# Both token tiles of a head in one pass through the attention, and one 256-column matmul for both parts of v

## The chip, the cores and the metric

The kernel runs on one core of one Trainium2 chip. The metric is the device time of one execution in microseconds; the median of three runs before the change is 2178.97 us (2178.82 to 2180.45).

## The reference

Two layers of a decoder over 256 tokens of 2048 features, in float32. Each layer runs an attention group and a convolution group side by side from one projection, joins them with one output projection, and ends in an MLP with a squared ReLU:

```python
for l in range(2):
    h = rmsnorm(x, attn_norm_g[l])
    q, k, v, gate_b, gate_c, conv_in = split(h @ w_in[l], ...)   # six parts of 1024 columns
    q, k = rmsnorm(q per map of 64), rmsnorm(k per map of 64)    # 8 heads, 2 maps each
    # differential attention of one head, blocks of 128 queries:
    s = (q_m . k_m) * scale + bias        # for both maps m, causal mask
    p = softmax(s[0]) - lam * softmax(s[1])
    attn = p @ v                          # v: 256 keys x 128
    attn = rmsnorm(attn, subln_g[l]) * (1 - lam_init)
    conv = gate_b * causal_conv3(gate_c * conv_in, conv_w[l])
    x = x + concat([attn, conv]) @ w_out[l]
    x = x + relu(rmsnorm(x) @ w_up[l])**2 @ w_down[l]
```

## The kernel before

Activations lie in SBUF in two token tiles of 128 tokens (`NT = 2`). Every float32 operand of a large matmul is split into a high part and a low part, and a product is made of three matmuls: high by high, high by low, low by high (`TERMS`). Weights stream in as `raw` tiles on SP's queue; ScalarE writes the high part (`whi`, line 282), VectorE the low part (`wlo`, line 283). `Weights.take` makes them three uses ahead.

TensorE runs in the order of the program (a manual schedule); the other engines' orders are settled by a scheduler when the program is built. The long stream on TensorE is the projections: in each layer q, k, v for heads 0 to 3 (512 columns each), q, k, v for heads 4 to 7, then gc and ci in turn (the convolution's inputs, four times 256 columns, `linear_t`, in which the weights stand still and high and low activations stream past in one 512-column matmul), then gb, then the output projection o. Between every few of these matmuls the code calls `work.tick()`. Side work is written as Python generators that yield how many ticks to wait; `Background` advances them at the ticks. So the attention of heads 0 to 3 is issued among the projections of heads 4 to 7 and that of heads 4 to 7 among gc and ci. A tick comes every six matmuls of 512 columns in q, k and v, and every four matmuls in gc and ci, so ticks are shorter there.

`attention` (line 486) runs eight units for a group of four heads, one for each token tile `t` and head `i`, all four heads of tile 0 first, started four ticks apart by `staggered`. A unit does:

- scores: for both maps three matmuls into a PSUM bank `sc` (line 500). A map has 64 features, so map 0 uses rows 0 to 63 of the array and map 1 rows 64 to 127. Tile 0 has 128 keys, tile 1 has 256.
- VectorE adds the bias and takes the maximum (line 503); ScalarE takes the exponential (510); VectorE forms the difference of the maps, `p` (521).
- nine ticks later: TensorE transposes `p` into a bank `ptp` (526); ScalarE and VectorE write its high and low parts, `pT` (528, 529).
- four ticks later: the product with v, three matmuls of 128 columns for each block of 128 keys (536), into a PSUM tile `av` that gathers the four heads of one token tile.
- with the fourth head: `av` is copied to `ao` (544), squared sums are taken on ScalarE (`asq`, 549), GpSimd makes the norm factors (`ams`, `a_e`, `a_r`, `af`, lines 551 to 554 and the helper's 380 and 382), VectorE scales (`an`, 556); nine ticks later TensorE transposes `an` into a bank `atp` (562) and ScalarE and VectorE write the two parts into `cat` (565, 566), which o reads.

PSUM has eight banks: two double banks for the projections (`mm`), three single banks in rotation (tag `bank`: `sc`, `ptp`, `atp` and others), and one for `av`. SBUF scratch of 512 columns comes from the pool `nat` (tag `wide`, seven buffers), scratch of the attention from `tmp`. The convolution (line 573 on) uses ScalarE, VectorE (579) and GpSimd (583) in the same stretch as the second group's attention. At the end of the mixer's scope its SBUF is reused by the MLP, whose first loads of w_up (`uraw`) wait on SP's queue for it.

Of the kernel before, what the change touches and what calls it, by code (L numbers as in the profile page):

```python
# [9 lines left out]
F32 = mybir.dt.float32  # L10
F32R = mybir.dt.float32r
AF = mybir.ActivationFunctionType
ALU = mybir.AluOpType
AX = mybir.AxisListType

P = 128
DEPTH = 2
D = 2048
S = 256
NT = S // P  # L20
AW = 1024
NH = 8
DK = 64
# [5 lines left out]
CH = 512  # L29
# [8 lines left out]
TERMS = ((0, 0), (0, 1), (1, 0))  # L38
# [46 lines left out]
def staggered(pieces, apart):  # L85

    entries = [[i * apart, p] for i, p in enumerate(pieces)]
    while entries:
        for e in list(entries):
            if e[0] <= 0:  # L90
                try:
                    e[0] = max(1, next(e[1]))
                except StopIteration:
                    entries.remove(e)
                    continue
            e[0] -= 1
        if entries:
            yield 1
# [3 lines left out]
def trunk(ctx: ExitStack, tc: tile.TileContext, x, w_in, w_out, conv_w, q_norm_g, k_norm_g,  # L102
          lambda_q1, lambda_k1, lambda_q2, lambda_k2, subln_g, attn_norm_g, mlp_norm_g,
          w_up, w_down, rel_bias, selector, out):
    nc = tc.nc
# [2 lines left out]
    xpool = ctx.enter_context(tc.tile_pool(name="xpool", bufs=1))  # L108
    apool = ctx.enter_context(tc.tile_pool(name="apool", bufs=4))
    wpool = ctx.enter_context(tc.tile_pool(name="wpool", bufs=3))  # L110
    nat = ctx.enter_context(tc.tile_pool(name="nat", bufs=7))
    small = ctx.enter_context(tc.tile_pool(name="small", bufs=4))
    dram = ctx.enter_context(tc.tile_pool(name="dram", bufs=1, space=bass.MemoryType.DRAM))
    mm = ctx.enter_context(tc.tile_pool(name="mm", bufs=2, space=PSUM))
    ps = ctx.enter_context(tc.tile_pool(name="ps", bufs=3, space=PSUM))
# [6 lines left out]
    def bank(name):  # L122
        return ps.tile([P, CH], F32, tag="bank", name=name)

    def wide(name):
        return nat.tile([P, CH], F32, tag="wide", name=name)
# [18 lines left out]
    ident = const.tile([P, P], F32, tag="ident", name="ident")  # L145
# [41 lines left out]
    s_gain = const.tile([P, DEPTH], F32, tag="sg", name="s_gain")  # L187
    nlam = const.tile([P, DEPTH], F32, tag="nlam", name="nlam")
# [188 lines left out]
    def rstd_of(ss, n, name, shape):  # L377

        e = small.tile([P, shape], F32, tag="rs_e", name=f"{name}_e")
        nc.gpsimd.tensor_scalar(e, ss, 1.0 / n, EPS, op0=ALU.mult, op1=ALU.add)  # L380
        r = small.tile([P, shape], F32, tag="rs_r", name=f"{name}_r")
        nc.gpsimd.tensor_tensor(r, e, mhalf[:, :shape], op=ALU.pow)
        return r
# [101 lines left out]

    def attention(l, qT, kT, v, h0, dst, bias, tmp):

        parts = dst.open()
        avs, r0s = {}, {}

        def unit(t, i):
            W = (t + 1) * P
            h = h0 + i
            s = tmp.tile([P, 2, S], F32, tag="s", name=f"s{h}_{t}")
            mx = small.tile([P, 2], F32, tag="mx", name=f"mx{h}_{t}")
            su = small.tile([P, 2], F32, tag="su", name=f"su{h}_{t}")
            for m in range(2):
                sc = bank(f"sc{h}_{t}_{m}")
                for n, (a, b) in enumerate(TERMS):
                    nc.tensor.matmul(  # L500
                        sc[:, :W], qT[m * DK:(m + 1) * DK, a, i, t * P:(t + 1) * P],
                        kT[m * DK:(m + 1) * DK, b, i, :W], start=(n == 0), stop=(n == 2))
                nc.vector.tensor_tensor_reduce(
                    out=s[:, m, :W], in0=sc[:, :W], in1=bias[:, 2 * h + m, S - W:],
                    op0=ALU.add, op1=ALU.max, scale=1.0, scalar=-3.0e38,
                    accum_out=mx[:, m:m + 1])
            nm = small.tile([P, 2], F32, tag="nm", name=f"nm{h}_{t}")
            nc.vector.tensor_scalar_mul(nm, mx, -1.0)
            for m in range(2):
                nc.scalar.activation(s[:, m, :W], s[:, m, :W], AF.Exp, bias=nm[:, m:m + 1],  # L510
                                     accum_out=su[:, m:m + 1])
            rc = small.tile([P, 2], F32, tag="rc", name=f"rc{h}_{t}")
            nc.vector.reciprocal(rc, su)
            if i == 0:
                r0s[t] = small.tile([P, 4], F32, tag="r0", name=f"r0_{h0}_{t}")
            nc.vector.tensor_copy(r0s[t][:, i:i + 1], rc[:, 0:1])
            c = small.tile([P, 1], F32, tag="c", name=f"c{h}_{t}")
            nc.vector.scalar_tensor_tensor(c, su[:, 0:1], rc[:, 1:2], nlam[:, l:l + 1],
                                           op0=ALU.mult, op1=ALU.mult)
            p = tmp.tile([P, S], F32, tag="p", name=f"p{h}_{t}", bufs=2)  # L520
            nc.vector.scalar_tensor_tensor(p[:, :W], s[:, 1, :W], c, s[:, 0, :W],
                                           op0=ALU.mult, op1=ALU.add)
            yield 9
            tp = bank(f"ptp{h}_{t}")
            for b in range(t + 1):
                nc.tensor.transpose(tp[:, b * P:(b + 1) * P], p[:, b * P:(b + 1) * P], ident)
            pT = tmp.tile([P, 2, S], F32R, tag="pT", name=f"pT{h}_{t}", bufs=2)
            nc.scalar.activation(pT[:, 0, :W], tp[:, :W], AF.Copy)
            nc.vector.tensor_sub(pT[:, 1, :W], tp[:, :W], pT[:, 0, :W].bitcast(F32))
            yield 4  # L530
            if i == 0:
                avs[t] = ps.tile([P, CH], F32, tag="av", name=f"av{h0}_{t}", bufs=1)
            av = avs[t]
            for k in range(t + 1):
                for n, (a, b) in enumerate(TERMS):
                    nc.tensor.matmul(  # L536
                        av[:, i * P:(i + 1) * P], pT[:, a, k * P:(k + 1) * P],
                        v[:, b, k, i * P:(i + 1) * P],
                        start=(k == 0 and n == 0), stop=(k == t and n == 2))
            if i < 3:  # L540
                return
            r0 = r0s[t]
            ao = wide(f"ao{h0}_{t}")
            nc.scalar.activation(ao, av, AF.Copy)
            ss = small.tile([P, 4], F32, tag="ams", name=f"ams{h0}_{t}")
            junk = wide(f"asq{h0}_{t}")
            for b in range(4):
                c = slice(b * P, (b + 1) * P)
                nc.scalar.activation(junk[:, c], ao[:, c], AF.Square, accum_out=ss[:, b:b + 1])
            for _ in range(2):  # L550
                nc.gpsimd.tensor_tensor(ss, ss, r0, op=ALU.mult)
            f = rstd_of(ss, P, f"a{h0}_{t}", 4)
            f2 = small.tile([P, 4], F32, tag="af2", name=f"af2{h0}_{t}")
            nc.gpsimd.tensor_tensor(f2, f, r0, op=ALU.mult)
            an = wide(f"an{h0}_{t}")
            nc.vector.tensor_tensor(
                an.rearrange("p (g d) -> p g d", d=P), ao.rearrange("p (g d) -> p g d", d=P),
                f2.unsqueeze(2).to_broadcast([P, 4, P]), op=ALU.mult)
            yield 9
            tp = bank(f"atp{h0}_{t}")  # L560
            for b in range(4):
                nc.tensor.transpose(tp[:, b * P:(b + 1) * P], an[:, b * P:(b + 1) * P], ident)
            tp3 = tp.rearrange("p (h c) -> p h c", c=P)
            hi = parts[:, 0, :, t * P:(t + 1) * P]
            nc.scalar.activation(hi, tp3, AF.Copy, scale=s_gain[:, l:l + 1])
            nc.vector.scalar_tensor_tensor(
                parts[:, 1, :, t * P:(t + 1) * P], tp3, s_gain[:, l:l + 1], hi.bitcast(F32),
                op0=ALU.mult, op1=ALU.subtract)

        yield from staggered([unit(t, i) for t in range(NT) for i in range(4)], 4)  # L570
        dst.ready = True

    def conv(l, q, u, cv, norm):
# [453 lines left out]
```

## Time and profile before

| | |
|---|---|
| median of three runs | 2178.97 us (2178.82 to 2180.45) |
| the profiled execution | 2181.14 us, span of its instructions 2179.4 us |
| TensorE matmuls, weight loads | 2156.6 us (99%), 1828.6 us (84%), 11066 each |
| VectorE, ScalarE, GpSimd | 1603.9 us (74%), 1271.7 us (58%), 138.8 us (6%) |
| attention group of heads 0 to 3, first layer | among q, k, v from 84.7 to 163.8 us |
| attention group of heads 4 to 7, first layer | among gc and ci from 164 to 213.5 us |
| TensorE clock granted | 0.999 |

In the rows of the profile, PE is TensorE, PEld its weight loads, DVE VectorE, ACT ScalarE, POOL GpSimd, SP the queue that issues most loads. A row of the groups gives line, engine, operation, output<-inputs with shapes, count, then busy time in us and the mean of one in ns, then the idle time of the engine before it and what ended it. A row of the chain in order of time, or of the timeline, starts with start and duration in us. In the chain, the duration runs to the next piece; in the timeline it is the instruction's own, and matmuls overlap.

### The profile page before, as it was taken

How to read it: one execution, taken by the hardware profiler on the slowest of the kernel's cores; microseconds unless marked ns; L12 is line 12 of the kernel's file. 1: busy time of each engine (PE TensorE's matmuls, PEld its weight loads, DVE VectorE, ACT ScalarE, POOL GpSimd, SP SyncE). 2: the span in 40 equal slices, each digit the busy share in tenths (PEclk: the TensorE clock that was granted, in tenths of full speed). 3: DMA queues.
4: the chain of work that ended last, by engine and by line, in shares of the span. 5: the costliest groups of instructions: out<-in, count | busy, mean ns of one | idle time of the engine just before them, and what ended most of it. 6: DMA issues, size and time to landing. Idle time of an engine off the chain costs nothing.

```text
span 2179.4 us, 29050 instructions
## 1 busy us (share of the span) xinstructions
PE 2156.6 (99%) x11066; PEld 1828.6 (84%) x11066; DVE 1603.9 (74%) x2229; ACT 1271.7 (58%) x1718; POOL 138.8 (6%) x194
## 2 busy tenths in 40 slices
PE   8999999999999999999999999999999999999999
PEld 6888888888888888888888888888888888888887
DVE  6677655698888888855566776557988888887554
ACT  6456445566666666654454654455666666665443
POOL 2021100000000000100011111000000000001000
PEclk9999999999999999999999999999999999999999
DMA  7555656476666666587565466656766666666774
GB/s 256 180 156 177 218 185 184 157 238 223 213 212 215 220 208 214 189 277 241 175 205 181 156 199 197 184 173 190 225 218 217 213 212 216 219 208 212 246 242 145
DMA packets 292491, 446.62 MB, mean 205 GB/s; under 512 B 10403, under 2 KB 191221, under 8 KB 292352
## 3 DMA queue, kind: packets, MB, share of 16 engines
q1 hardware_dynamic: 285648, 423.66, 61.5%
q0 software_dynamic: 6656, 21.10, 2.6%
q8 instruction: 86, 1.41, 0.3%
q14 instruction: 53, 0.43, 0.1%
q10 hardware_dynamic: 48, 0.02, 0.0%
HBM read 425.84 MB, written 18.90 MB: 204 GB/s over the span
## 4 chain that ended last, share of the span: by engine, by line
PE 94%; DMA 2%; DVE 2%; ACT 1%; issue 1%; SPq 0%; DVEq 0%; ACTq 0%
PE upc L809 29%; PE dn L969 15%; PE pr L849 13%; PE o L338 8%; PE q L338 4%; PE gc L360 4%; PE ci L360 4%; PE k L338 4%; PE gb L360 4%; PE v L338 4%; PE upw L809 1%; DMA uraw<-in_w_up_dram 1%; PE sc L500 1%; PE av L536 1%; PE tpn L402 1%; DMA draw<-in_w_down_dram 1%
## 5 line engine op out<-in xcount | busy, mean ns | idle before, releaser
L283 DVE TENSOR_TENSOR wlo<-raw,whi 128x1024 fp32r<-128x1024 f32 (+1 forms) x386 | 473.3, 1228 | 385.5 <-ACT whi L282 381.0
L282 ACT ACTIVATE whi<-raw 128x1024 fp32r<-128x1024 f32 (+1 forms) x386 | 406.8, 1055 | 477.8 <-PE dn L969 166.7
L809 PE MATMUL upc<-nT,uhi 128*128 128x512 f32 x1920 | 477.5, 391 | 0.0
L694 ACT ACTIVATE uhi<-uraw 128x1024 fp32r<-128x1024 f32 x256 | 271.2, 1060 | 287.3 <-PE upc L809 253.9
L809 PEld LDWEIGHTS upc<-nT,uhi 128*128 128x128 f32 x1920 | 352.7, 188 | 68.2
L695 DVE TENSOR_TENSOR ulo<-uraw,uhi 128x1024 fp32r<-128x1024 f32 x256 | 312.8, 1222 | 115.3 <-ACT uhi L694 112.9
L969 PE MATMUL dn<-whi,g 128*128 128x512 f32 x1024 | 316.4, 389 | 0.0
L809 PEld LDWEIGHTS upc<-nT,ulo 128*128 128x128 f32 x1920 | 261.9, 190 | 18.7
L809 PE MATMUL upc<-nT,ulo 128*128 128x256 f32 x1920 | 267.7, 282 | 0.0
L969 PEld LDWEIGHTS dn<-whi,g 128*128 128x128 f32 x1024 | 192.2, 188 | 39.7
L969 PE MATMUL dn<-wlo,g 128*128 128x512 f32 x512 | 199.6, 390 | 1.1 <-DVE wlo L283 1.0
L338 PE MATMUL o<-whi,cat 128*128 128x512 f32 x512 | 159.6, 390 | 0.0
L969 PEld LDWEIGHTS dn<-wlo,g 128*128 128x128 f32 x512 | 96.1, 188 | 22.6 <-DVE wlo L283 2.8
L338 PEld LDWEIGHTS o<-whi,cat 128*128 128x128 f32 x512 | 96.2, 188 | 19.7
L338 PE MATMUL o<-wlo,cat 128*128 128x512 f32 x256 | 99.6, 389 | 0.0
L831 POOL DMA_DIRECT2D hid<-h x64 | 34.9, 545 | 949.1 <-ACT h L830 913.4
L849 PE MATMUL pr<-t13h,f 128*128 128x512 f32 x240 | 93.8, 391 | 0.0
L338 PE MATMUL q<-whi,nT 128*128 128x512 f32 x256 | 86.4, 406 | 4.1 <-ACT nT L248 4.1
L338 PE MATMUL k<-whi,nT 128*128 128x512 f32 x256 | 85.3, 399 | 0.0
L849 PE MATMUL pr<-t24h,f 128*128 128x512 f32 x240 | 84.0, 391 | 0.0
L849 PE MATMUL pr<-b2h,f 128*128 128x512 f32 x240 | 84.0, 391 | 0.0
L338 PE MATMUL v<-whi,nT 128*128 128x512 f32 x256 | 83.4, 396 | 0.0
(330 smaller groups left out, 3431.0 us busy)
## 6 DMA issues: line engine op xcount, KB each, us to landing
uraw<-in_w_up_dram SPq DMA_DIRECT2D x128, 1024.0 KB, 5.9
raw<-in_w_in_dram SPq DMA_DIRECT2D x192, 512.0 KB, 3.9
draw<-in_w_down_dram SPq DMA_DIRECT2D x64, 1024.0 KB, 5.1
raw<-in_w_down_dram SPq DMA_DIRECT2D x64, 1024.0 KB, 5.7
raw<-in_w_out_dram SPq DMA_DIRECT2D x64, 512.0 KB, 3.6
hid<-h POOLq DMA_DIRECT2D x64, 256.0 KB, 4.3
back<-hid SPq DMA_DIRECT2D x32, 512.0 KB, 3.3
rev<-by_dist_d POOLq DMA_DIRECT2D x4, 1024.0 KB, 11.1
```

Source lines behind the costliest of these rows:

```text
L282: nc.scalar.activation(hi[:, k], raw[:, k], AF.Copy)
L283: nc.vector.tensor_sub(lo[:, k], raw[:, k], hi[:, k].bitcast(F32))
L338: nc.tensor.matmul(acc[:, t], a.ap[:, pa, k % KG, t * P:(t + 1) * P], (hi, lo)[pw][:, j], start=(k == 0 and n == 0), stop=(k == nk - 1 and ...
L360: nc.tensor.matmul(acc[:, f, 0] if part else acc[:, f], wt[:, k % 4, fs], a.ap[:, 0, k % KG] if part else a.ap[:, :, k % KG], start=(part ...
L402: nc.tensor.transpose(tp[:, i * S + t * P:i * S + (t + 1) * P], xs[n][:, t, k * P:(k + 1) * P], ident)
L500: nc.tensor.matmul(sc[:, :W], qT[m * DK:(m + 1) * DK, a, i, t * P:(t + 1) * P], kT[m * DK:(m + 1) * DK, b, i, :W], start=(n == 0), stop=(n ...
L694: nc.scalar.activation(hi, src, AF.Copy)
L695: nc.vector.tensor_sub(lo, src, hi.bitcast(F32))
L809: nc.tensor.matmul(acc[:, 0] if part else acc, wt[:, k], a.ap[:, 0, k % KG] if part else a.ap[:, :, k % KG], start=(part == 0 and kh == 0 ...
L831: nc.gpsimd.dma_start(hid[i // 2][:, i % 2 * 2 * S:(i % 2 + 1) * 2 * S], u)
L849: nc.tensor.matmul(prods[n], fs[j][:, pa, a], b[pw], start=(j == 0 and m == 0), stop=(stop and m == 2))
L969: nc.tensor.matmul(acc[:, t], f[:, pa, k, t * P:(t + 1) * P], (hi, lo)[pw][:, k % 2], start=(b == 0 and k == 0 and m == 0), stop=(b == NB2 ...
```

## The change

A unit is now a head with both its token tiles: four units for a group, started eight ticks apart.

- The twelve score matmuls are issued together, the maps alternating; both tiles share the bank of their map (columns 0 to 127 tile 0, 128 to 383 tile 1). The exponentials, sums and differences are written side by side into one tile `s`, and `p` takes the place of its first map.
- One bank `ptp` takes all three transposes, and one pass each makes the high and the low part `pT`.
- The product with v: the high part of the probabilities meets both parts of v in one matmul of 256 columns, the low part meets the high part of v in one of 128. `av` holds one head: for each tile the sum and, beside it, the share of v's low part. ScalarE copies that share to `low`, VectorE adds it to the rest into `ao`.
- With the fourth head, both tiles are normalised one after the other, and nine ticks later both are transposed one after the other.
- Buffers: `nat` six and not seven, `s` two larger ones and not three, `pT` one and not two, `ao` in `tmp`; `av` one for each head.

```diff
-    nat = ctx.enter_context(tc.tile_pool(name="nat", bufs=7))
+    nat = ctx.enter_context(tc.tile_pool(name="nat", bufs=6))
...
-        def unit(t, i):
-            W = (t + 1) * P
+        OFF = (0, P)
+        r0 = small.tile([P, 4, NT], F32, tag="r0", name=f"r0_{h0}")
+        ao = tmp.tile([P, NT, CH], F32, tag="ao", name=f"ao{h0}", bufs=1)
+
+        def unit(i):
...
-            for m in range(2):
-                sc = bank(f"sc{h}_{t}_{m}")
-                for n, (a, b) in enumerate(TERMS):
...
+            sc = [bank(f"sc{h}_{m}") for m in range(2)]
+            for t in range(NT):
+                W = (t + 1) * P
+                for n, (a, b) in enumerate(TERMS):
+                    for m in range(2):
+                        nc.tensor.matmul(
+                            sc[m][:, OFF[t]:OFF[t] + W],
+                            qT[m * DK:(m + 1) * DK, a, i, t * P:(t + 1) * P],
+                            kT[m * DK:(m + 1) * DK, b, i, :W], start=(n == 0), stop=(n == 2))
...
             yield 9
-            tp = bank(f"ptp{h}_{t}")
-            for b in range(t + 1):
+            tp = bank(f"ptp{h}")
+            for b in range(3):
                 nc.tensor.transpose(tp[:, b * P:(b + 1) * P], p[:, b * P:(b + 1) * P], ident)
...
             yield 4
-            for k in range(t + 1):
-                for n, (a, b) in enumerate(TERMS):
-                    nc.tensor.matmul(
-                        av[:, i * P:(i + 1) * P], pT[:, a, k * P:(k + 1) * P],
-                        v[:, b, k, i * P:(i + 1) * P],
-                        start=(k == 0 and n == 0), stop=(k == t and n == 2))
+            av = ps.tile([P, CH], F32, tag="av", name=f"av{h}", bufs=1)
+            av = av.rearrange("p (t n c) -> p t n c", t=NT, n=2)
+            for t in range(NT):
+                for k in range(t + 1):
+                    w = slice(OFF[t] + k * P, OFF[t] + (k + 1) * P)
+                    nc.tensor.matmul(av[:, t], pT[:, 0, w], v[:, :, k, i * P:(i + 1) * P],
+                                     start=(k == 0), stop=False, skip_group_check=True)
+                    nc.tensor.matmul(av[:, t, 0], pT[:, 1, w], v[:, 0, k, i * P:(i + 1) * P],
+                                     start=False, stop=(k == t), skip_group_check=True)
+            low = nat.tile([P, NT, P], F32, tag="wide", name=f"avl{h}")
+            nc.scalar.activation(low, av[:, :, 1], AF.Copy)
+            nc.vector.tensor_add(ao[:, :, i * P:(i + 1) * P], av[:, :, 0], low)
             if i < 3:
                 return
...
+            for t in range(NT):
...
+                an = wide(f"an{h0}_{t}")
...
+                an_.append(an)
             yield 9
-            tp = bank(f"atp{h0}_{t}")
...
+            for t in range(NT):
+                tp = bank(f"atp{h0}_{t}")
+                for b in range(4):
+                    nc.tensor.transpose(tp[:, b * P:(b + 1) * P], an_[t][:, b * P:(b + 1) * P],
+                                        ident)
...
-        yield from staggered([unit(t, i) for t in range(NT) for i in range(4)], 4)
+        yield from staggered([unit(i) for i in range(4)], 8)
```

More of the change, by code (lines that the diff above doesn't have):

```diff
@@ L488, in attention @@
         parts = dst.open()
-        avs, r0s = {}, {}
-        def unit(t, i):
-            W = (t + 1) * P
+        OFF = (0, P)
+        r0 = small.tile([P, 4, NT], F32, tag="r0", name=f"r0_{h0}")
+        ao = tmp.tile([P, NT, CH], F32, tag="ao", name=f"ao{h0}", bufs=1)
+        def unit(i):
             h = h0 + i
-            s = tmp.tile([P, 2, S], F32, tag="s", name=f"s{h}_{t}")
-            mx = small.tile([P, 2], F32, tag="mx", name=f"mx{h}_{t}")
-            su = small.tile([P, 2], F32, tag="su", name=f"su{h}_{t}")
-            for m in range(2):
-                sc = bank(f"sc{h}_{t}_{m}")
-                for n, (a, b) in enumerate(TERMS):
[L500 to L512, printed above, removed]
-            nc.vector.reciprocal(rc, su)
[L514 to L522, printed above, removed]
@@ new lines, in unit @@
+            s = tmp.tile([P, 2, 3 * P], F32, tag="s", name=f"s{h}", bufs=2)
+            mx = small.tile([P, NT, 2], F32, tag="mx", name=f"mx{h}")
+            su = small.tile([P, NT, 2], F32, tag="su", name=f"su{h}")
+            sc = [bank(f"sc{h}_{m}") for m in range(2)]
+            for t in range(NT):
+                W = (t + 1) * P
+                for n, (a, b) in enumerate(TERMS):
+                    for m in range(2):
[3 more added lines that the diff above has]
+                            kT[m * DK:(m + 1) * DK, b, i, :W], start=(n == 0), stop=(n == 2))
@@ new lines, in unit @@
+            for t in range(NT):
+                W = (t + 1) * P
+                for m in range(2):
+                    nc.vector.tensor_tensor_reduce(
+                        out=s[:, m, OFF[t]:OFF[t] + W], in0=sc[m][:, OFF[t]:OFF[t] + W],
+                        in1=bias[:, 2 * h + m, S - W:], op0=ALU.add, op1=ALU.max, scale=1.0,
+                        scalar=-3.0e38, accum_out=mx[:, t, m:m + 1])
+            nm = small.tile([P, NT, 2], F32, tag="nm", name=f"nm{h}")
+            nc.vector.tensor_scalar_mul(nm, mx, -1.0)
@@ new lines, in unit @@
+            for t in range(NT):
+                for m in range(2):
+                    e = s[:, m, OFF[t]:OFF[t] + (t + 1) * P]
+                    nc.scalar.activation(e, e, AF.Exp, bias=nm[:, t, m:m + 1],
+                                         accum_out=su[:, t, m:m + 1])
+            rc = small.tile([P, NT, 2], F32, tag="rc", name=f"rc{h}")
+            nc.vector.reciprocal(rc, su)
+            nc.vector.tensor_copy(r0[:, i], rc[:, :, 0])
+            c = small.tile([P, NT], F32, tag="c", name=f"c{h}")
@@ L523, in unit @@
+            p = s[:, 0]
+            for t in range(NT):
+                w = slice(OFF[t], OFF[t] + (t + 1) * P)
+                nc.vector.scalar_tensor_tensor(c[:, t:t + 1], su[:, t, 0:1], rc[:, t, 1:2],
+                                               nlam[:, l:l + 1], op0=ALU.mult, op1=ALU.mult)
+                nc.vector.scalar_tensor_tensor(p[:, w], s[:, 1, w], c[:, t:t + 1], s[:, 0, w],
+                                               op0=ALU.mult, op1=ALU.add)
             yield 9
-            tp = bank(f"ptp{h}_{t}")
@@ L525, in unit @@
-            for b in range(t + 1):
+            tp = bank(f"ptp{h}")
+            for b in range(3):
                 nc.tensor.transpose(tp[:, b * P:(b + 1) * P], p[:, b * P:(b + 1) * P], ident)
-            pT = tmp.tile([P, 2, S], F32R, tag="pT", name=f"pT{h}_{t}", bufs=2)
-            nc.scalar.activation(pT[:, 0, :W], tp[:, :W], AF.Copy)
-            nc.vector.tensor_sub(pT[:, 1, :W], tp[:, :W], pT[:, 0, :W].bitcast(F32))
+            pT = tmp.tile([P, 2, 3 * P], F32R, tag="pT", name=f"pT{h}", bufs=1)
@@ L530, in unit @@
+            nc.scalar.activation(pT[:, 0], tp[:, :3 * P], AF.Copy)
+            nc.vector.tensor_sub(pT[:, 1], tp[:, :3 * P], pT[:, 0].bitcast(F32))
             yield 4
-            if i == 0:
-                avs[t] = ps.tile([P, CH], F32, tag="av", name=f"av{h0}_{t}", bufs=1)
-            av = avs[t]
-            for k in range(t + 1):
-                for n, (a, b) in enumerate(TERMS):
-                    nc.tensor.matmul(
-                        av[:, i * P:(i + 1) * P], pT[:, a, k * P:(k + 1) * P],
-                        v[:, b, k, i * P:(i + 1) * P],
-                        start=(k == 0 and n == 0), stop=(k == t and n == 2))
+            av = ps.tile([P, CH], F32, tag="av", name=f"av{h}", bufs=1)
@@ new lines, in unit @@
+            av = av.rearrange("p (t n c) -> p t n c", t=NT, n=2)
+            for t in range(NT):
+                for k in range(t + 1):
[4 more added lines that the diff above has]
+                                     start=False, stop=(k == t), skip_group_check=True)
@@ L540, in unit @@
+            low = nat.tile([P, NT, P], F32, tag="wide", name=f"avl{h}")
+            nc.scalar.activation(low, av[:, :, 1], AF.Copy)
+            nc.vector.tensor_add(ao[:, :, i * P:(i + 1) * P], av[:, :, 0], low)
             if i < 3:
                 return
[L542 to L558, printed above, removed]
@@ L559, in unit @@
-            yield 9
-            tp = bank(f"atp{h0}_{t}")
[L561 to L568, printed above, removed]
@@ L570, in attention @@
-        yield from staggered([unit(t, i) for t in range(NT) for i in range(4)], 4)
+            an_ = []
+            for t in range(NT):
+                ss = small.tile([P, 4], F32, tag="ams", name=f"ams{h0}_{t}")
+                junk = wide(f"asq{h0}_{t}")
+                for b in range(4):
+                    c = slice(b * P, (b + 1) * P)
+                    nc.scalar.activation(junk[:, c], ao[:, t, c], AF.Square,
+                                         accum_out=ss[:, b:b + 1])
+                for _ in range(2):
+                    nc.gpsimd.tensor_tensor(ss, ss, r0[:, :, t], op=ALU.mult)
+                f = rstd_of(ss, P, f"a{h0}_{t}", 4)
+                f2 = small.tile([P, 4], F32, tag="af2", name=f"af2{h0}_{t}")
+                nc.gpsimd.tensor_tensor(f2, f, r0[:, :, t], op=ALU.mult)
+                an = wide(f"an{h0}_{t}")
+                nc.vector.tensor_tensor(
+                    an.rearrange("p (g d) -> p g d", d=P),
+                    ao[:, t].rearrange("p (g d) -> p g d", d=P),
+                    f2.unsqueeze(2).to_broadcast([P, 4, P]), op=ALU.mult)
+                an_.append(an)
@@ new lines, in unit @@
+            yield 9
+            for t in range(NT):
+                tp = bank(f"atp{h0}_{t}")
+                for b in range(4):
+                    nc.tensor.transpose(tp[:, b * P:(b + 1) * P], an_[t][:, b * P:(b + 1) * P],
+                                        ident)
+                tp3 = tp.rearrange("p (h c) -> p h c", c=P)
+                hi = parts[:, 0, :, t * P:(t + 1) * P]
+                nc.scalar.activation(hi, tp3, AF.Copy, scale=s_gain[:, l:l + 1])
+                nc.vector.scalar_tensor_tensor(
+                    parts[:, 1, :, t * P:(t + 1) * P], tp3, s_gain[:, l:l + 1], hi.bitcast(F32),
+                    op0=ALU.mult, op1=ALU.subtract)
```

## The prediction

> **What bounds the kernel now.** I read the first part of the page (busy time by engine), then its chain of the work that ended last, then that chain in order of time inside the attention stages, and last single stretches of the timeline.
>
> ```profile
> span 2179.4 us, 29050 instructions
> ...
> PE 2156.6 (99%) x11066; PEld 1828.6 (84%) x11066; DVE 1603.9 (74%) x2229; ACT 1271.7 (58%) x1718; POOL 138.8 (6%) x194
> ...
> PE 94%; DMA 2%; DVE 2%; ACT 1%; issue 1%; SPq 0%; DVEq 0%; ACTq 0%
> ```
>
> TensorE works 99% of the span and is 94% of the chain. So an instruction taken from TensorE comes off the time, and a wait put on TensorE goes onto it. Other engines matter only where TensorE comes to wait for them.
>
> The attention has no stage of its own. Its instructions are dropped, at fixed places written by hand, between the matmuls of other projections: heads 0 to 3 among the q, k and v projections of the second half, heads 4 to 7 among gc and ci. The chain in order of time shows what one drop costs, from its start to the next instruction:
>
> ```profile
> 177.26 0.49 PE sc L500 x6
> 177.75 0.67 PE gc L360 x4
> 178.42 0.28 PE av L536 x3
> 178.71 0.13 PE ptp L526
> ...
> 181.15 0.56 PE sc L500 x6
> ...
> 194.39 0.62 PE av L536 x6
> 195.02 0.24 PE ptp L526 x2
> ...
> 265.65 44.69 PE gb L360 x256
> ```
>
> sc are the scores, ptp the transposes of the probabilities, av the product with v; the smaller count is token tile 0, the larger tile 1. The gb row is the undisturbed pace: sixteen matmuls, eight of 512 columns and eight of 256, take 2.79 us. Further down the row of ci gives twenty (the same sixteen and four of 512) in 3.72, so 0.23 for 512 columns and 0.117 for 256. The four 256-column matmuls behind the scores therefore ought to take 0.47 and take 0.67: 0.20 is paid each time TensorE leaves the scores.
>
> **What the change takes off TensorE.**
>
> *Scores.* The twelve matmuls of a head are now one drop and no longer two. Before: 0.49 + 0.56 + 2 x 0.20 = 1.45 us. How long three more steps in one drop take is seen in the timeline of one drop, asked for in ever narrower windows, so that only the later matmuls are left:
>
> ```profile
> 114.14 0.62 PE L500 MATMUL sc<-kT,qT 64*128 64x256 f32 x6
> 114.37 0.40 PE L500 MATMUL sc<-kT,qT 64*128 64x256 f32 x4
> 114.48 0.28 PE L500 MATMUL sc<-kT,qT 64*128 64x256 f32 x2
> ```
>
> The six go in three pairs, started 0.23 and 0.11 apart. The two maps of a head thus overlap already, on the two halves of the rows, and alternating them in the program adds nothing. A later pair costs 0.11, so the new drop is 0.49 + 3 x 0.11 + 0.20 = 1.02 and 0.43 is saved. If the pairs kept the mean of a drop (0.56/3), only the second 0.20 would go. I take 0.40, as the middle step was seen directly.
>
> *Probabilities times v.* Nine matmuls of 128 columns (0.28 + 0.62 = 0.90, so 0.10 each) become three of 256 and three of 128: 3 x 0.117 + 3 x 0.10 = 0.65. 0.25 is saved (0.15 if all six take 0.125, 0.30 if the wide ones cost no more than the narrow ones). The halves of v lie apart in memory, but gb streams its two parts in the same way at the pace above.
>
> *Transposes.* 0.13 + 0.24 against 0.13 + 2 x 0.11: 0.02. Those of the finished heads (atp) are entered four times and not eight; 0.3 in all, an estimate from the sizes above.
>
> Per head 0.67; sixteen heads (two layers) 10.7, with atp **11.0 us** (bounds 5.6 and 12.4).
>
> **What it puts on TensorE.** Before, tile 0 of a group of four heads was finished, normalised and transposed well ahead of tile 1. Now both tiles end together, and the program puts both sets of four atp transposes directly behind each other, nine steps behind the last av. In the second group these steps are short, and this is where I expect new waits, in each layer.
>
> ```profile
> 206.51 2.83 PE gc L360 x16
> 209.33 3.72 PE ci L360 x20
> 213.06 0.44 PE atp L562 x4
> ```
>
> The last av ends at 206.51. From there to atp there are 36 matmuls, 2.83 + 3.72 = 6.55 us, and the changed program has the same 36. What must be done meanwhile:
>
> ```profile
> 203.06 2.16 POOL L583 TENSOR_TENSOR cv<-cv,rowb 128x512 f32<-128x512 f32 x1 [8.19 <-ACT whi L282]
> 208.53 0.48 POOL L551 TENSOR_TENSOR ams<-ams,r 128x4 f32<-128x4 f32 x2 [3.32 <-ACT asq L549]
> ...
> 210.46 0.33 POOL L554 TENSOR_TENSOR af<-a_r,r 128x4 f32<-128x4 f32 x1
> ```
>
> ```profile
> L283 DVE TENSOR_TENSOR wlo<-raw,whi 128x1024 fp32r<-128x1024 f32 (+1 forms) x386 | 473.3, 1228 | 385.5 <-ACT whi L282 381.0
> ```
>
> ```profile
> L566 DVE SCALAR_TENSOR_TENSOR cat<-atp,s_gain,cat 128x512 fp32r<-128x512 f32 x8 | 6.0, 748 | 0.4
> ...
> L556 DVE TENSOR_TENSOR an<-ao,af 128x512 f32<-128x512 f32 x8 | 5.5, 690 | 0.4
> ...
> L579 DVE SCALAR_TENSOR_TENSOR cv<-gc00w,gains,cv 128x255 f32<-128x255 f32 x2 | 0.9, 480 | 0.0
> ```
>
> ```profile
> L565 ACT ACTIVATE cat<-atp,s_gain 128x512 fp32r<-128x512 f32 x8 | 5.5, 690 | 6.9 <-PE atp L562 6.9
> ```
>
> *First wait.* In the built program GpSimd has the convolution's product (cv) ahead of the norm factors of the attention, and VectorE comes to it through a weight split (0.6 to 1.23 of it left), four convolution steps (4 x 0.48) and the new addition of the low half (about 0.4, an estimate from the 0.48 of L521 at 256 elements, shown below). That is 2.9 to 3.5, then cv 2.16, the norm factors 208.53 to 210.79 = 2.26, and an 0.69: 8.0 to 8.6 us against 6.55. I take 1.8. It is 0 if GpSimd does the factors first, 2.5 with slow handovers.
>
> *Second wait.* On VectorE's list the eviction of the first atp set (cat) stands ahead of the second an. So the second set, wanted 0.44 behind the first, must wait for its transposes, cat on ScalarE, cat on VectorE and an: 0.44 + 0.69 + 0.75 + 0.69 = 2.57. The wait is 2.1, with handovers 2.2.
>
> *Third.* At the start of gc the two atp sets of the first group and the two banks of scores share three PSUM banks, so the second score bank waits for cat of the first set, queued behind a weight split (1.23) on VectorE. Bounds 0 and 1; I take 0.5.
>
> 4.5 a layer, **9.0 us** in all (bounds 1 and 12). What is queued behind the waiting transposes on TensorE is the whole projection ci; nothing else suffers, since the weights run ahead.
>
> **Costed at nothing.** VectorE and ScalarE lose instructions (one pass for two tiles) and stay under TensorE. The pool of wide tiles falls from 7 to 6 and the probabilities' copies from two buffers to one; each is free again several steps before its next use. On SP's queue the three loads of w_up move two w_in loads later; TensorE waits for no load in these stages, and if they came late it would be seen there as a wait on whi.
>
> **Sum.** -11.0 + 9.0 = -2.0. The profiled execution took 2181.14 us (span 2179.4, 1.7 around it), so 2179.1 by it. It lies 0.1% above the median 2178.97 of the three runs, which gives **2177.0 us**. About 0.2% (4.4 us) is what a measurement of this kernel can tell from no change.
>
> **Rivals.**
>
> *The new waits do not come* (0.22). The factors are ready in time, or cat does not hold up the second an. Then nearly all of the 11 stays, less the small third wait: 2168.5. For it speaks that the present trace has no such wait, against it that the two lists have a fixed order and that the second chain has no slack in it at all.
>
> *The probabilities come late* (0.12), the slower side. Scores, softmax and difference now run for both tiles before the first transpose.
>
> ```profile
> 186.07 0.48 DVE L521 SCALAR_TENSOR_TENSOR p<-s,c 128x256 f32<-128x256 f32 x1
> ```
>
> ```profile
> L503 DVE CUSTOM_DVE_ANT_0 s<-sc,bias 128x128 f32<-128x128 f32 x32 | 8.2, 286 | 2.9 <-PE sc L500 2.9
> ```
>
> ```profile
> L510 ACT ACTIVATE s<-s,nm 128x128 f32<-128x128 f32 x32 | 12.5, 393 | 13.8 <-DVE nm L508 13.8
> ```
>
> The scores of 181.15 had their p at 186.55, 5.4 us later. The other tile adds 0.28 of scores, two reads (0.57), two exponentials (0.79) and a p of at most 0.48: 7.5, or 8 with the short steps between. TensorE's way to the transposes in the second group is 0.82 + 0.67 + 0.35 + 2.79 + 0.65 + 2.3 + 0.82 + 0.67 = 9.1 us. It decides at 9.1: one more weight split (1.23) inside the chain still nearly fits, two make it 1.4 late. On eight heads (second group, two layers) with the rest of the forecast that is some +9: 2186.
>
> *A cold TensorE* (0.12). Two waits of about 2 us with 0.44 us of work between them are new. The trace has one long wait and one of such a length:
>
> ```profile
> 9.90 0.80 PE L338 MATMUL q<-whi,nT 128*128 128x512 f32 x1 [4.09 <-ACT nT L248]
> ...
> 10.92 1.05 PE L338 MATMUL q<-whi,nT 128*128 128x512 f32 x2
> ```
>
> ```profile
> 412.32 2.12 PE L809 MATMUL up<-nT,uhi 128*128 128x512 f32 x8 [1.97 <-ACT ev L819]
> ```
>
> After 4.09 us a 512-column matmul takes over 0.4 (two in 1.05), nearly twice 0.23; after 1.97 us eight take 2.12, full pace. If the two waits together act like the long one, some twelve matmuls of ci lose 0.2 each, 2.5 us a layer: 2182. [...]
>
> **How the numbers follow.** The forecast has 0.54 and by the bounds of its terms runs from 2172 to 2181. The range takes in most of the first rival and the cold clock: 2168 to 2183; left out are the late probabilities and the lower edge of the first rival. Faster: the first rival and a tenth of the forecast, 0.28. Slower: the late probabilities a third of the cold clock and a last hundredth of the forecast, 0.17. The rest, 0.55, is within 0.2%.
>
> **What would show it.** In the changed profile: sc x12 at about 0.8 us and av x6 at about 0.65 in the chain; TensorE waiting for an in both layers, once about 1.8 and once about 2.2 us, between gc01 and ci01; the first group shorter by over 2.5 us in each layer, the second no shorter at all. It is wrong if TensorE waits for p (ptp) or for pT, if whi or wlo appear among its releasers in these stages, or if the atp transposes follow without a gap.

## The result, and the profile after

The changed kernel takes **2185.49 us** (median of 8 runs, 2183.05 to 2187.28), the kernel before 2179.34 on the same chip (8 runs, 2178.82 to 2181.89): ratio 1.0026, 95% interval 1.0016 to 1.0035. It is slower, by some 6 us. The forecast was 2177.0, its range ended at 2183.

The profiled execution took 2186.76 us. The first lines of its page:

```profile
span 2185.0 us, 28897 instructions
...
PE 2151.1 (98%) x11018; PEld 1825.6 (84%) x11018; DVE 1598.0 (73%) x2181; ACT 1268.6 (58%) x1710; POOL 140.4 (6%) x194
```

TensorE is busy for 5.5 us less than before, and the span is 5.6 us longer: TensorE now stands still for 11 us more. The page can't say where. The chain of the work that ended last, in order of time inside the second group of heads (start, length, what), first shows the new drops:

```profile
178.52 0.88 PE sc L504 x12
179.40 0.67 PE ci L360 x4
180.07 0.33 PE ptp L536 x3
180.40 2.80 PE ci L360 x16
183.20 0.12 PE av L547
183.32 0.06 PE av L549
...
183.78 0.06 PE av L549
183.84 2.26 PE ci L360 x11
```

One drop of scores takes 0.88 and again makes the four narrow matmuls behind it 0.20 slow (0.67 for 0.47): 1.08 for 1.45 before, 0.37 saved a head. The six matmuls of av take 0.64 for 0.90, the transposes 0.33 for 0.37. That is 0.67 a head, 10.7 us in all. Some 15 us later the chain leaves TensorE:

```profile
198.19 0.57 PE gc L360 x3
198.76 0.88 ACT asq L562 x6
199.64 1.35 issue
200.99 1.29 POOL cv L601
202.28 1.15 POOL ams L565
...
206.22 0.21 POOL af L568
...
206.46 0.70 DVE an L570
...
207.21 0.67 PE atp L579 x4
...
207.90 0.69 ACT cat L583
...
208.62 0.30 DVE cat L584
208.92 0.36 issue
209.29 0.69 DVE an L570
...
210.02 1.12 PE atp L579 x4
211.14 5.08 PE ci L360 x18
```

Read from the top, this is the prediction's first wait (the last av ends at 198.19, then the convolution's product on GpSimd, the norm factors, an, and only then atp), and below it the second (cat on ScalarE, cat on VectorE, the second an). The list of what TensorE waited for (in all, times, longest) gives the sums:

```profile
PE atp L579 <- DVE an L570: 9.5, 4, 2.7
...
PE sc L504 <- DVE cat L584: 0.6, 2, 0.3
```

Four waits for an, 2.44 and 2.16 us in layer 0, 2.72 and 2.16 in layer 1. But the last two lines of the chain hold something else. Four transposes took 0.67 the first time and 1.12 the second, and 18 matmuls of ci then took 5.08, where the kernel before does 20 in 3.72. The windows of this stretch (stretch, its length, busy PE with the number of matmuls, granted clock, DMA share and GB/s) say why:

```profile
201.40:204.81 3.41, 3.37 (x19) 1.00 0.23 73
204.81:208.23 3.42, 0.66 (x4) 1.00 0.86 269
208.23:211.64 3.41, 1.62 (x6) 0.50 0.18 56
211.64:215.05 3.41, 3.41 (x13) 0.50 0.97 274
```

From 208.23 to 215.05 the granted clock is at half. The edges of these stretches are those of the trace's clock record: the changes in it lie whole multiples of 3.41 us apart (the stretch at full clock between the two layers' half ones is 1075.2 us, 315 times 3.413, each half one 6.83, twice that). I call 3.41 us a step; here two steps in a row are at half, in layer 1 as well (from 1290.25 us). In the kernel before, the clock is at full from 15.83 us to 2176.47, where TensorE has no more work.

### The profile page after: what moved, and what is told of

Read it like the earlier page. It is cut to its first block, busy times and chain, and to the rows that moved or that the text cites. A ratio compares the mean times of both kernels' runs of the same rounds, so it can differ in the third digit from the quotient of the medians.

```text
span 2185.0 us, 28897 instructions
## 1 busy us (share of the span) xinstructions
PE 2151.1 (98%) x11018; PEld 1825.6 (84%) x11018; DVE 1598.0 (73%) x2181; ACT 1268.6 (58%) x1710; POOL 140.4 (6%) x194
## 4 chain that ended last, share of the span: by engine, by line
PE 92%; DVE 3%; DMA 3%; ACT 1%; issue 1%; POOL 1%; SPq 0%; DVEq 0%; ACTq 0%
PE upc L827 29%; PE dn L987 15%; PE pr L867 13%; PE o L338 8%; PE ci L360 4%; PE q L338 4%; PE gb L360 4%; PE v L338 4%; PE k L338 4%; PE gc L360 3%; DMA uraw<-in_w_up_dram 2%; DVE ulo L713 1%; PE sc L504 1%; DMA back<-hid 1%; PE tpn L402 1%
```

## The experiments

All are timed against the kernel before; ratios are to it, with their 95% interval. **Theory A** is that the merged pass gains what was forecast and that the waits for an, with the half clock that they bring, take it back and more. **Theory B** is that the loss lies in the merged pass itself, so that taking the waits away only moves it.

**e1_later: the second group's transposes nine steps later.**

```
-            yield 9
+            yield 9 if h0 == 0 else 18
             for t in range(NT):
                 tp = bank(f"atp{h0}_{t}")
```

> The changed kernel, with the transposes of the finished heads in the second group 18 ticks behind the last product with v, and not 9. Theory A (the loss is the two waits of TensorE for the normalised heads, 2.4 to 2.7 and 2.16 us in each layer, and the half clock of 6.8 us that follows them, some 3 us in each layer): no wait, granted clock 1.00 throughout, about 2170 us against 2185.5 for the changed kernel and 2179.3 for the one before. Theory B (the loss is in the merged pass itself and the waits only show it; they come up at another place): 2180 to 2185 us, with new waits of like size later in ci or in o.

2171.85 us, ratio 0.9965 (0.9953 to 0.9978). The timeline of TensorE (a wait would stand in brackets) shows both sets at once, no wait, and ci at full pace:

```profile
208.35 2.01 PE L360 MATMUL ci<-nT,whi 128*128 128x512 f32 x8
210.20 1.04 PE L579 MATMUL atp<-ident,an 128*128 128x128 f32 x8
210.99 1.20 PE L360 MATMUL ci<-nT,wlo 128*128 128x256 f32 x8
```

One number in the program turns 6 us lost into 8 us gained. Theory B falls.

**e3_filler: the same waits, but TensorE busy in them.** In the second group seven matmuls whose result nothing uses stand ahead of each set.

```
                 tp = bank(f"atp{h0}_{t}")
+                if h0:
+                    for n in range(7):
+                        nc.tensor.matmul(tp, qT[:, 0, 0, 0:P], v[:, 0, 0], start=True, stop=True)
```

> The changed kernel, with seven matmuls of 512 columns (1.6 us) whose results nobody uses issued ahead of each of the two sets of transposes in the second group; the sets overwrite them. What TensorE waits for is unchanged, so the time from the last matmul of ci to the second set stays as long, but TensorE works for most of it. If the half clock costs some 3 us a layer of its own: clock 1.00 and 2185.5 - 6 = about 2179.5 us. If the clock costs nothing beside the waits: 2185.5 us. If the filler lengthens the path: above that.

2180.48 us, ratio 1.0002 (0.9993 to 1.0011). TensorE still gets past this point only when an is there, but the clock stays at full (1.000 over the profiled span), and 5.0 us of the 13.6 between the changed kernel and e1_later are gone (5.2 by the ratios, whose intervals allow some 2.4 to 8). The other 8.6 are mostly the waits. The rows give the price of the half clock more closely. From the start of the second set to the start of gb it is 57.89 us in layer 0 and 56.98 in layer 1 of the changed kernel, 55.60 in both of e3_filler; in layer 1 the two sets are also 3.28 apart for 2.82. So the half clock alone costs 2.3 and 1.8 us, 4.1 in all.

**e2_apart: only the first wait is left.** The second set goes five steps behind the first, in both groups.

```
             for t in range(NT):
+                if t:
+                    yield 5
                 tp = bank(f"atp{h0}_{t}")
```

> The changed kernel, with five ticks between the two sets of transposes of the finished heads, in both groups. The first wait (2.4 to 2.7 us a layer) should stay, the second (2.16) be covered by the matmuls of ci that now stand between. Theory A with a clock that drops only when the two waits come close together: clock 1.00, 2185.5 - 4.3 - 6 = about 2175 us. If one wait of this length is enough to drop the clock: about 2181 us. Theory B: no better than 2183 us.

2177.48 us, ratio 0.9989 (0.9980 to 0.9997), between the two expectations. The list of waits has the first ones only, and the windows show one step at half clock instead of two:

```profile
PE atp L581 <- DVE an L570: 5.2, 2, 2.7
```

```profile
203.47:206.88 3.41, 0.97 (x7) 1.00 0.85 257
206.88:210.30 3.42, 3.42 (x14) 0.50 0.21 62
210.30:213.71 3.41, 3.41 (x22) 1.00 0.97 273
```

So behind one wait of 2.44 us the clock was at half for one step (206.88 to 210.30 us). It wasn't so in every execution: of 11 executions six had a mean clock of 0.998, four 0.999 and one 1.000, with mean times of 2177.97, 2176.94 and 2175.57. One half step takes 0.0008 off this mean (half of 3.41 us in 2177). The half clock behind TensorE's last work counts too, and gives 0.999 by itself in the profile of the kernel before (from 2176.47 to the span's end at 2179.4 us). So 1.000 means no half step amid the work, 0.999 one at most, and 0.998 two, as in the profiled execution, or one and nearly a whole one at the end.

**e5_short: the same single wait, shortened by five unused matmuls.**

```
                 tp = bank(f"atp{h0}_{t}")
+                if h0 and t == 0:
+                    for n in range(5):
+                        nc.tensor.matmul(tp, qT[:, 0, 0, 0:P], v[:, 0, 0], start=True, stop=True)
```

(on top of e2_apart)

> The two sets of atp stand apart as in e2_apart, so that one wait per layer is left (2.44 and 2.7 us there), and five matmuls of 512 columns whose result nothing uses fill the first 1.13 us of it. TensorE comes past this point no earlier, but it idles for 1.3 to 1.6 us only. The clock records of the runs so far change in steps of 3.413 us; every such step after which the clock was at half had at least 1.8 us of idle TensorE in it, and none with 1.75 us or less was followed by half clock. Theory A (waits, and the half clock that they bring by their share of such a step): the clock stays at full in both layers, about three quarters of the half-clock stretches of e2_apart (each 3.41 us long, so up to 1.7 us lost) are gone, 2175.0 us. Theory B (the clock is not what is left in e2_apart): same as e2_apart, 2177.5 us.

2174.52 us, ratio 0.9975 (0.9966 to 0.9985); the mean clock was 1.000 in nine executions of ten. TensorE waits for nothing less, it is only idle for less, and 3.0 us go. The expectation had 2.5, which the intervals don't tell from 3.0. The rows agree: from the start of the first set to the start of gb it is 57.59 and 57.42 us in the two layers of e2_apart, 56.03 and 56.02 here, 3.0 in all, so some 1.5 us for one half step. In layer 1 the step that holds the shortened wait leaves the clock at full:

```profile
1281.34:1284.76 3.42, 1.83 (x9) 1.00 0.66 215
1284.76:1288.17 3.41, 3.41 (x22) 1.00 0.16 58
```

**e9_pair: both waits in place, none of them long.** Five unused matmuls ahead of the first set, two ahead of the second.

```
                 tp = bank(f"atp{h0}_{t}")
+                if h0:
+                    for n in range(2 if t else 5):
+                        nc.tensor.matmul(tp, qT[:, 0, 0, 0:P], v[:, 0, 0], start=True, stop=True)
```

> The changed kernel with both waits for atp kept in their place and shortened by matmuls of 512 columns whose result nothing uses: five ahead of the first set (wait 1.3 to 1.6 us), two ahead of the second (wait 1.7 us, 0.9 us of work between them). TensorE comes past this point as in the changed kernel; only how long it idles differs. No wait alone is as long as 1.75 us, the most idle time in a clock step of 3.413 us that the runs so far left at full clock. If it is the length of one wait that lowers the clock, it stays at full: 2180.5 us as e3_filler. If it is the share of idle time in a step, the two waits add up wherever they fall into one step, by the phase some six times in ten: mean clock 0.999 or 0.998 in most executions, some 1.2 steps of 3.41 us at half clock in each, 2182.4 us. Theory B (neither matters): 2185.5 us as the changed kernel.

2182.88 us, ratio 1.0013 (1.0004 to 1.0022). The clock was at 0.998 in six of 11 executions, 0.999 in four, 1.000 in one. No wait for an is longer than 1.7 us, while a single one of 1.75 us in the up projection of e2_apart left the clock at full, so the length of one wait doesn't tell these cases apart. The time is nearer to the 2182.4 expected for the share of idle time than to the 2180.5 for the length; by the intervals alone it would not decide. The windows of both layers, on the steps of the clock record:

```profile
204.68:208.09 3.41, 1.91 (x10) 1.00 0.79 256
208.09:211.50 3.41, 1.90 (x13) 1.00 0.24 60
```

```profile
1286.70:1290.12 3.42, 1.47 (x9) 1.00 0.28 99
1290.12:1293.53 3.41, 3.41 (x14) 0.50 0.62 172
```

In layer 0 the edge of a step falls between the two waits, each step is busy for 1.9 us of 3.41, and the clock stays. In layer 1 the whole second wait (1.70 us) and the last 0.25 of the first fall into one step, busy for 1.47, and the next is at half. The step ahead of it holds the rest of the first wait and is busy for 2.08.

**e4_narrow: e1_later with the nine narrow matmuls for the product with v.**

```
-                    nc.tensor.matmul(av[:, t], pT[:, 0, w], v[:, :, k, i * P:(i + 1) * P],
...
+                    for n, (a, b) in enumerate(TERMS):
+                        nc.tensor.matmul(av[:, t, 0], pT[:, a, w],
+                                         v[:, b, k, i * P:(i + 1) * P],
+                                         start=(k == 0 and n == 0), stop=(k == t and n == 2))
-            low = nat.tile([P, NT, P], F32, tag="wide", name=f"avl{h}")
...
+            nc.scalar.activation(ao[:, :, i * P:(i + 1) * P], av[:, :, 0], AF.Copy)
```

> The kernel with the later transposes, and the product with v again as nine matmuls of 128 columns for a head, summed in one place, so that the copy and the addition of the low share go too. By the prediction's term (0.25 us a head, sixteen heads) 4 us above the kernel with the later transposes, by its bounds 2.4 to 4.8. If the wide matmul saves nothing, the same as that kernel.

2176.57 us, ratio 0.9981 (0.9972 to 0.9990): 4.7 us over e1_later by the medians, 3.5 by the ratios, 0.22 to 0.29 a head. By the rows the nine take 0.96 us, 0.32 more than the six. The time isn't clean: in the profiled execution a wait of 1.87 us in the up projection of layer 1, which the edit doesn't touch, has a half step behind it.

**e7_split: e1_later with the scores of a head in two drops again.**

```
             for t in range(NT):
+                if t:
+                    yield 2
                 W = (t + 1) * P
```

> e1_later with the scores of a head in two drops again (token tile 0, and tile 1 two steps later), all else merged. It measures the largest term of the prediction alone: 0.40 us a head for one drop in place of two, so 6.4 us, 2178.3 us. If only the cost of leaving the scores once (0.20) is saved: 3.2, 2175.1 us. By what the narrow product with v took back (4.7 of the 8.3 us between e1_later and the kernel before) some 4 us would be left for it, 2176.

2179.41 us, ratio 0.9999 (0.9990 to 1.0008), 7.4 us over e1_later by the ratios (4 to 11 by their intervals), more than any of the three expectations. The list of waits shows that it isn't all the drop:

```profile
PE sc L506 <- DVE cat L586: 1.8, 2, 0.9
...
PE av L551 <- DVE pT L541: 1.0, 2, 0.5
```

The wait on cat was 0.6 in e1_later, that on pT not there: 2.2 us are new waits, some 5.2 are left for sixteen drops more, 0.33 a head. The edit was no clean separation, as it also moves the steps behind it.

**e6_mapwise: e1_later with the scores written map by map.**

```
-                for n, (a, b) in enumerate(TERMS):
-                    for m in range(2):
+                for m in range(2):
+                    for n, (a, b) in enumerate(TERMS):
```

> e1_later with the score matmuls of a tile written map by map (three of the first map, then three of the second) and no longer alternating. The prediction read from the drops before that the two maps overlap on the two halves of the rows in either order: then same time as e1_later, 2171.9 (within 1 us). If alternating is what pairs them in the changed kernel, a drop costs up to 0.43 us more, on sixteen heads 6.9: 2178.7 us.

2171.53 us, ratio 0.9960 (0.9947 to 0.9972). The same as e1_later within the intervals, and a drop is 0.89 long instead of 0.88. (The wait for cat, 0.6 us in e1_later, isn't in its list.) Alternating the maps does nothing.

**e8_both: e1_later with the first group's transposes five steps later too.**

```
-            yield 9 if h0 == 0 else 18
+            yield 14 if h0 == 0 else 18
```

> e1_later, and in the first group of heads the two atp sets five steps later too (behind the first scores of the second group), so that these scores don't meet cat of the first set on the three PSUM banks. Theory A: the wait of 0.3 us a layer on the second score bank goes, 0.6 us in all: 2171.2 us, which its interval won't tell from e1_later; the list of waits will show whether it is gone. Theory B: no change, or a new wait where atp now stands.

2170.84 us, ratio 0.9957 (0.9945 to 0.9970). TensorE no longer waits for cat; the gain over e1_later is inside both intervals. It has the lowest median here, 8.7 us under the kernel before. Where the attention of layer 1 begins (first q of its second half) and ends (first gb), by the chains of the kernel before, of the changed kernel and of e8_both:

```profile
1165.55 4.08 PE q L338 x18
...
1346.31 13.73 PE gb L360 x78
```

```profile
1167.93 4.08 PE q L338 x18
...
1351.09 9.07 PE gb L360 x51
```

```profile
1159.58 4.08 PE q L338 x18
...
1335.02 2.07 PE gb L360 x10
```

180.76, 183.16 and 175.44 us: with the waits gone the merged attention of this layer is 5.3 us shorter. In layer 0 the same stretch is 180.76, 183.30 and 176.00 us, 4.8 shorter; there TensorE waits 0.4 us for a weight split (whi) in e8_both. That is 10.1 in all. As the changed kernel has it, the attention is 2.4 to 2.5 us a layer longer.

## Why the prediction was wrong, point by point

**The gain was right.** 11.0 forecast; 10.7 by the rows of a drop, 10.1 by the stages in e8_both, 10.5 without its wait for a weight. By terms: scores 0.37 a head (forecast 0.40; e7_split, disturbed, 0.33), av 0.26 (forecast 0.25; e4_narrow, which also changes what evicts it, 0.22 to 0.32), ptp 0.04 (0.02). What was costed at nothing cost nothing: neither whi, wlo nor p is among TensorE's waits in these stages in the changed kernel. In layer 0 the first group is shorter by 3.3 us (75.6 for 78.9, from the first q to the first gc), the second longer by 5.9.

**The waits were there, where they were put, and somewhat larger.** First wait 1.8 forecast, 2.44 and 2.72 measured. The start of cv, 2.8 and 3.1 us behind the last av, fits the 2.9 to 3.5 forecast. The term that was too small is what GpSimd then does, 2.16 + 2.26 forecast from the rows before. It was 1.29 + 4.15 in layer 0 (cv from 200.99, ams from 202.28, af ended at 206.43) and 2.38 + 3.06 in layer 1, both 1.0 more. So the factors alone grew by 1.9 and 0.8. Single operations among them took about 1 us longer than before, different ones in the two layers (in layer 0 the two of ams, 1.46 for 0.48, and a_r, 2.08 for 1.01; in layer 1 a_e, 1.15 for 0.19); why is open. Second wait 2.2, measured 2.16 twice. Third 0.5, 0.3 in the list. Together 10.1 for 9.0.

**The step that failed is the clock.** The forecast set it at nothing and gave the cold clock as a rival 0.12. The size in that rival was about right: 2.5 us a layer there, 2.3 and 1.8 by the rows of e3_filler, 5.0 for two by its time. Its mechanism was right in part: it had the two waits act together, but e2_apart shows that one is enough. What was wrong is the reasoning that made it unlikely. I had read the length of a wait: 1.97 us at full pace in the kernel before, 4.09 at half. That the length decides was my assumption; the trace didn't show it. The wait of 4.09 us shows nothing of the kind. The transposes ahead of it took 2.01, and eight of the same kind later, at full pace, 1.03, so TensorE was at half pace before that wait began:

```profile
3.81 2.01 PE L402 MATMUL tpn<-ident,x 128*128 128x128 f32 x8
...
21.87 1.03 PE L402 MATMUL tpn<-ident,x 128*128 128x128 f32 x8
```

And the windows on the clock's own steps show that the wait of 1.97 us was spared by its place. This is the stretch of the kernel before, in which that wait lies:

```profile
408.36:411.78 3.42, 1.99 (x13) 1.00 1.02 384
411.78:415.19 3.41, 2.87 (x16) 1.00 0.50 173
```

The wait is cut by an edge, and its larger part leaves the step busy for 1.99 of 3.42. At the same line of the program a wait of 1.8 us in e8_both (layer 1) fell into one step, and one of 1.75 in e2_apart (layer 0) left its step busy a little longer:

```profile
1478.40:1481.81 3.41, 1.58 (x11) 1.00 1.02 377
1481.81:1485.23 3.42, 3.42 (x10) 0.50 0.30 105
```

```profile
408.27:411.68 3.41, 1.66 (x9) 1.00 0.91 323
411.68:415.10 3.42, 3.42 (x21) 1.00 0.09 34
```

Behind the step busy for 1.66 us the clock was at full, behind the one busy for 1.58 at half. The steps at full clock amid the work that are given here with less than 2 us of busy TensorE, in order of it: 0.66 and 1.27 (the changed kernel, the second from 1286.84 us), 0.97 (e2_apart), 1.47 (e9_pair) and 1.58 (e8_both) had half clock behind them; 1.66 (e2_apart), 1.83 (e5_short), 1.90 and 1.91 (e9_pair) and 1.99 (the kernel before) full clock. The edge isn't sharper than that: at the end of e8_both a step with 1.58 (from 2164.48 us) has a full one behind it. By these figures the two new waits had hardly a way out: of 2.44 and 2.16 us of idle time with 0.67 of work between them, one step holds at least 2.3, wherever its edges fall, so it is busy for 1.1 at most. So the half clock was no rival with 0.12; with the waits in place it was to be expected. (The forecast's own 1.8 and 2.2 give at least 2.0 idle and at most 1.4 busy, so by the same figures it followed from those as well.) The kernel before has no step amid its work that is busy for less than 1.99 us, so its trace left the matter open; it gave little reason to call the half clock unlikely.

The sum by what was measured: -10.7 + 10.1 + 4.1 = +3.5, or +4.4 with the 5.0 by time. One small term is missing in it: four transposes that come straight from a wait take 0.67 and not 0.44, some 0.9 us for the four sets. That makes +4.4 to +5.3. The attention stages of the two profiles are 2.5 and 2.4 us longer, 4.9 in all, and the interval of the ratio is +3.5 to +7.6 us. What is left of the 5.6 us between the two spans lies outside the attention; the two profiles also differ by about 1 us in the up projection and at the start, which the change doesn't touch (waits of 3.2 and 2.5 us in all for ev in the up projection, of 4.1 and 2.7 for the first nT, of 3.5 and 4.6 ahead of the first matmul).

**The rivals.** The late probabilities did not come: no wait for p or pT in the changed kernel. The new waits did come, so that rival falls as well.

## What to carry to other kernels

Merging two passes on the busiest engine saves what its rows say, but it also makes two ends meet that were apart before; cost the chain from the last product to the first consumer on every engine in it, and move the consumer back by as many steps as that chain is longer than the work in between. Idle gaps on TensorE were not to be judged one by one here: amid the work the half clock came behind steps of 3.41 us with 1.83 us or more of idle time in them (busy for 1.58 or less), in one gap or two, and not behind those with 1.75 or less. So add up the idle time of neighbouring gaps, and where it comes near these figures, put a step at half clock (1.4 to 1.6 us in e2_apart) into the price as a risk. Where the time of two versions differs by more than their waits explain, look at the granted clock in windows of 3.41 us before looking for another wait.

## What the runs showed of the hardware

- The granted clock of TensorE changed only at edges whole multiples of 3.41 us apart (6.83 and 1075.2 us in the changed kernel). Behind a step at full clock that was busy for 1.58 us or less it was at half (once at full, at the end of e8_both), behind one with 1.66 or more at full, as far as the steps given above go. Half steps amid the work are in five traces: behind the waits for an in the changed kernel, e2_apart and e9_pair, in the up projection in e4_narrow and e8_both. The edges lay differently in the two profiled executions: full clock is recorded from 13.67 us on in the changed kernel and from 15.83 in the kernel before. Whether issued matmuls or time made the difference isn't shown; busy time here has modelled ends.
- Equal executions differed: with the same instructions e2_apart had a mean clock of 0.998, 0.999 or 1.000. A half step cost 1.6 us in layer 0 of e2_apart, where TensorE was busy for all of it, and 1.4 in layer 1 (57.59 and 57.42 us against 56.03 and 56.02 in e5_short).
- Unused matmuls ahead of a wait made a kernel faster: five of 0.23 us in each layer, 3.0 us less in all (e2_apart to e5_short, by the medians and by the rows).
